# Moving the pool of the experts' tiles up by 128 bytes in SBUF

## The chip, the cores and the metric

The kernel runs on one core of one Trainium2 chip. The metric is the device time of one execution in microseconds (us); a comparison takes the median of several runs. Engines are called as the profile calls them: PE is TensorE's matmul, PEld its weight load, DVE is VectorE, ACT is ScalarE, POOL is GpSimd, SP is SyncE, whose queue issues the DMAs.

## The reference

Two decoder layers over 256 tokens of 1024 channels, then a final RMSNorm. Each layer has four groups of attention heads behind one input projection, an output projection, and a SwiGLU channel mixer: dense in layer 0, eight experts with the two best of them for each token in layer 1. The part that the change touches is the mixture:

```
logits = (xt @ router).astype(jnp.float32)
top_v, top_i = lax.top_k(logits, TOP_K)
gates = jax.nn.softmax(top_v, axis=-1)
...
y = (jax.nn.silu(xb @ w1[e]) * (xb @ w3[e])) @ w2[e]
return y * g[:, None].astype(y.dtype)
```

`w1` and `w3` of an expert are 1024 x 3584, `w2` is 3584 x 1024, all fp32: the eight experts have 352 MB of weights.

## The kernel before

Every product of fp32 operands is made of three matmuls. Each operand is split in a high part (rounded to the format that PE multiplies in one pass) and a low part (what is left), and high x high, high x low and low x high are summed in PSUM. `mm3` (L453 to L456) issues the three: `o, lh, rh`, then `o, lh, rl`, then `o, ll, rh`, the first operand stationary, the second moving. Since the trace names the operands as moving, then stationary, `acc<-wh,g` is a matmul in which a split weight `wh` streams past a stationary `g`.

The weights are split on the core. `Stream` (L217 on) loads units of 1 MB from HBM into tiles `raw`; for each half of one, a piece of 128 x 1024, ACT copies it to a tile `wh` (L305) and DVE subtracts that from `raw` into `wl` (L306). There are five `wh` and five `wl` tiles, and up to fifteen `raw` slots. A load is issued as soon as a `raw` slot is free; a piece is split up to four ahead of the matmuls that read it (`MAHEAD`).

The work of the experts is 56 steps, 8 experts by 7 blocks of 512 hidden channels. Stationary in the experts are small tiles of the pool `moe` (called `mp`, L1013): `g` holds the high and low part of the tokens gathered for an expert (128 slots), `th` and `tl` the hidden block transposed; `sT` holds the expert's slots to put the results back, `yy` the expert's output, `hd` and `sg` the hidden block. One step is

- `g1`: the gate and the up product, 4 pieces each, 6 matmuls of 512 columns on a piece (`acc<-wh,g`, `acc<-wl,g`); ahead of the up product `hidden` transposes the block of the step before with four small matmuls (`tp<-cst,hd`, L1239);
- `g2`: the down product of the step before, 4 pieces, 6 matmuls of 512 columns on each (`mm<-wh,th`, `mm<-wl,th`, `mm<-wh,tl`).

That is 72 matmuls of 512 columns a step. Once for each expert come two bursts of gather matmuls (L1187) and a transposition in `back`, and four scatters of two matmuls each (`tp<-yy,sT`, L1292) from the expert before. The order of all this is written out by hand: the layers and the experts run in the order of the program on each engine.

SBUF is laid out by pools, one after the other from the low end: `rawp`, `hp` (the `wh`), `lp` (the `wl`), `com` (constants and small tiles), then in layer 1's mixture `mp` and `ms` (small statistics). Other pools stand at the high end, among them `big` with `xh` and `xl`, the split activations of the layers. `com` holds a tile `fill` that nothing reads (L1388); its size decides where the tiles behind it begin. In the built program the byte addresses in a partition are:

```
tiles                                   start      modulo 512   modulo 256
wh, wl (all ten)                        74368 ...     128          128
xh, xl (stationary or moving, layers)  188288 ...     384          128
cTh, cTl (stationary, layers)          133120 ...       0            0
th, tl of the dense mixer (moving)     165632 ...     256            0
cst (identity for transposes)          115456         256            0
g of the experts, both buffers         117504 ...     256            0
th, tl of the experts                  174848 ...     256            0
```

A matmul reads whole blocks of these tiles, at steps of 512 bytes or a multiple, so a tile's place modulo 256 is that of every operand cut from it, but for the 416-column products of the layers.

Two functions issue nearly all matmuls in question: `mm3` for those in the experts and in the layers' `proj_nat` (moving `wh`, stationary `xh`: the same shape and order as in the experts, with `xh` in place of `g`), and `accumulate` and the loops of `g1` in `ffn0` for the dense mixer, where the weights are stationary and 256 columns of `xh` or `th` move.

Of the kernel before, what the change touches and what calls it, by code (L numbers as in the profile page):

```python
# [24 lines left out]
F32 = mybir.dt.float32  # L25
# [302 lines left out]
def trunk(ctx, tc, a, out, stop=None):  # L328
# [7 lines left out]
    com = ctx.enter_context(tc.tile_pool(name="com", bufs=1, reuse_waits="tile"))  # L336
# [1048 lines left out]

    rg = com.tile([128, KC, E], F32, name="rg")
    trib = com.tile([128, 128], BF, name="trib")
    com.tile([128, 8], F32, name="fill")  # L1388
    onesb = com.tile([128, 1], BF, name="onesb")
    pool.memset(onesb, 1.0)  # L1390
    ffn0()
# [55 lines left out]
```

## Time and profile before

| what | value |
|---|---|
| three runs | 1491.73, 1489.2, 1486.29 us; median 1489.2 us |
| the profiled execution's own time | 1487.16 us |
| its span on the core | 1485.0 us |
| mean granted TensorE clock | 0.994 |
| busy: PE, PEld, DVE, ACT, POOL | 99%, 84%, 83%, 71%, 2% of the span |
| chain that ended last | PE 96% |
| layer 0 with the dense mixer | about 0 to 320 us |
| attention of layer 1 | about 320 to 455 us |
| the experts and the final norm | from about 455 us to the end |

A matmul's own duration in the trace (395 ns for 512 columns) reaches past the start of the next one, since matmuls are pipelined. What a matmul costs in a stream is the distance from its start to the next start; it is read from the starts in the view in order of time. Rows of that view have the start in us, the duration in us, the engine, line, operation, operands, array size and moving shape.

### The profile page before, as it was taken

What the parts mean: (1) busy time and instruction counts of PE and PEld (TensorE: products, weight loads), DVE (VectorE), ACT (ScalarE), POOL (GpSimd) and SP (SyncE); (2) the same over time, 40 slices, a digit from 0 to 9 for tenths busy, and PEclk for the clock granted to TensorE, in tenths of its full rate; (3) what the DMA queues carried; (4) which work ended last, traced back from release to release, by engine and by line L of the source; (5) the groups of instructions that cost most, each with busy time, mean ns of one, the idle gap of its engine ahead of it and who ended that gap; (6) DMA issues with size and microseconds to landing.
All of it is one profiled execution on the core that took longest, in us unless ns stands there. A gap on an engine that the chain in (4) does not pass through costs nothing.

```text
span 1485.0 us, 21467 instructions
## 1 busy us (share of the span) xinstructions
PE 1464.4 (99%) x8092; PEld 1254.0 (84%) x8092; DVE 1229.9 (83%) x1574; ACT 1047.0 (71%) x1387; POOL 31.9 (2%) x38
## 2 busy tenths in 40 slices
PE   9999999999999999999999999999999999999996
PEld 7999999999997788888888888888888888888885
DVE  6766655666756998998998999899899989989996
ACT  6666444455656877777777777778787777777774
POOL 2001000010000100000000000000000000000000
PEclk9999999999999999999999999999999999999998
DMA  9723555366538798999999999899999999999770
GB/s 368 290 86 135 182 179 191 135 217 223 187 117 317 306 381 303 347 367 331 361 349 339 354 350 370 324 352 362 336 357 354 360 330 346 366 332 360 235 256 31
DMA packets 62334, 426.36 MB, mean 287 GB/s; under 512 B 7176, under 2 KB 7824, under 8 KB 13712
## 3 DMA queue, kind: packets, MB, share of 16 engines
q1 hardware_dynamic: 62224, 424.92, 78.2%
q8 instruction: 65, 1.06, 0.3%
q14 instruction: 45, 0.37, 0.1%
HBM read 423.85 MB, written 1.05 MB: 286 GB/s over the span
## 4 chain that ended last, share of the span: by engine, by line
PE 96%; DVE 1%; ACT 1%; DMA 0%; issue 0%; SPq 0%; POOL 0%; ACTq 0%; POOLq 0%
PE acc L454 14%; PE acc L456 14%; PE acc L455 14%; PE mm L454 7%; PE mm L456 7%; PE mm L455 7%; PE B L972 3%; PE B L971 3%; PE B L970 3%; PE A L522 2%; PE A L523 2%; PE A L524 2%; PE tp L1187 2%; PE tp L1239 2%; PE A L594 2%; PE A L595 1%
## 5 line engine op out<-in xcount | busy, mean ns | idle before, releaser
L306 DVE TENSOR_TENSOR wl<-raw,wh 128x1024 fp32r<-128x1024 f32 (+2 forms) x801 | 970.8, 1224 | 155.9 <-ACT wh L305 152.6
L305 ACT ACTIVATE wh<-raw 128x1024 fp32r<-128x1024 f32 (+2 forms) x801 | 844.5, 1057 | 301.5 <-PE acc L456 123.3
L454 PE MATMUL acc<-wh,g 128*128 128x512 f32 x896 | 360.3, 402 | 0.0
L455 PE MATMUL acc<-wl,g 128*128 128x512 f32 x896 | 353.9, 395 | 0.3 <-DVE wl L306 0.3
L456 PE MATMUL acc<-wh,g 128*128 128x512 f32 x896 | 354.2, 395 | 0.0
L456 PEld LDWEIGHTS acc<-wh,g 128*128 128x128 f32 x896 | 169.1, 189 | 39.5
L455 PEld LDWEIGHTS acc<-wl,g 128*128 128x128 f32 x896 | 169.5, 189 | 36.9 <-DVE wl L306 0.7
L454 PEld LDWEIGHTS acc<-wh,g 128*128 128x128 f32 x896 | 169.4, 189 | 36.2
L454 PE MATMUL mm<-wh,th 128*128 128x512 f32 x440 | 173.8, 395 | 0.0
L456 PE MATMUL mm<-wh,tl 128*128 128x512 f32 x440 | 173.7, 395 | 0.0
L455 PE MATMUL mm<-wl,th 128*128 128x512 f32 x440 | 173.6, 395 | 0.0
L456 PEld LDWEIGHTS mm<-wh,tl 128*128 128x128 f32 x440 | 82.8, 188 | 19.6 <-DVE tl L460 0.3
L455 PEld LDWEIGHTS mm<-wl,th 128*128 128x128 f32 x440 | 82.9, 188 | 19.5
L454 PEld LDWEIGHTS mm<-wh,th 128*128 128x128 f32 x440 | 82.9, 188 | 19.3
L972 PE MATMUL B<-xh,wl 128*128 128x256 f32 x336 | 95.2, 283 | 0.0
L970 PE MATMUL B<-xh,wh 128*128 128x256 f32 x336 | 95.1, 283 | 0.0
L971 PE MATMUL B<-xl,wh 128*128 128x256 f32 x336 | 95.1, 283 | 0.0
L970 PEld LDWEIGHTS B<-xh,wh 128*128 128x128 f32 x336 | 64.5, 192 | 0.0
L972 PEld LDWEIGHTS B<-xh,wl 128*128 128x128 f32 x336 | 64.5, 192 | 0.0
L971 PEld LDWEIGHTS B<-xl,wh 128*128 128x128 f32 x336 | 64.5, 192 | 0.0
L594 PE MATMUL A<-xh,wh 128*128 128x256 f32 x176 | 51.4, 292 | 0.0
L596 PE MATMUL A<-xh,wl 128*128 128x256 f32 x176 | 49.7, 283 | 0.0
(256 smaller groups left out, 1745.8 us busy)
## 6 DMA issues: line engine op xcount, KB each, us to landing
raw<-in_wmoe SPq DMA_DIRECT2D x324, 1024.0 KB, 6.0
raw<-in_wt SPq DMA_DIRECT2D x53, 1024.0 KB, 4.9
raw<-in_wmoe SPq DMA_DIRECT2D x24, 512.0 KB, 4.9
ac<-in_att SPq DMA_DIRECT2D x2, 1728.0 KB, 8.5
raw<-in_wt SPq DMA_DIRECT2D x5, 512.0 KB, 4.7
raw<-in_wt SPq DMA_DIRECT2D x2, 960.0 KB, 14.6
raw<-in_wt SPq DMA_DIRECT2D x2, 928.0 KB, 8.6
raw<-in_wt SPq DMA_DIRECT2D x2, 832.0 KB, 9.0
```

Source lines behind the costliest of these rows:

```text
L305: nc.scalar.activation(h[:, sl], raw[:, sl], AF.Copy)
L306: nc.vector.tensor_sub(l[:, sl], raw[:, sl], h[:, sl].bitcast(F32))
L454: pe.matmul(o, lh, rh, start=start, stop=False, **kw)
L455: pe.matmul(o, lh, rl, start=False, stop=False, **kw)
L456: pe.matmul(o, ll, rh, start=False, stop=stop, **kw)
L522: pe.matmul(o, wh[wsl], h, start=s0, stop=False, skip_group_check=True)
L523: pe.matmul(o, wh[wsl], lo, start=False, stop=False, skip_group_check=True)
L594: pe.matmul(o, hv[:, k], xh[:, k], start=k == 0, stop=False)
L596: pe.matmul(o, lv[:, k], xh[:, k], start=False, stop=k == KC - 1)
L970: pe.matmul(o, hv[:, k], xh[:, k], start=k == 0, stop=False)
L971: pe.matmul(o, hv[:, k], xl[:, k], start=False, stop=False)
L972: pe.matmul(o, lv[:, k], xh[:, k], start=False, stop=k == KC - 1)
```

## The change

The tile `fill` in the pool `com` gets 40 numbers instead of 8, so 160 bytes instead of 32 in each partition.

```diff
     trib = com.tile([128, 128], BF, name="trib")
-    com.tile([128, 8], F32, name="fill")
+    com.tile([128, 40], F32, name="fill")
     onesb = com.tile([128, 1], BF, name="onesb")
```

All that stands behind it at the low end moves up by 128 bytes: `onesb`, every tile of `mp` (`g` to 117632, `th` to 174976, so 128 modulo 256 and 384 modulo 512, and with them `yy`, `xx`, `xnh`, `xnl`, `hd`, `oh`, `sg`, `sT`, `tl` and three early `raw` slots) and every tile of `ms`. `wh`, `wl`, `cst`, the regular `raw` tiles and everything of the layers and the dense mixer stay where they are. No instruction is added, removed or moved on any engine; only addresses differ.

## Rows read from the trace of the kernel before

**Rows 1.** The page, busy us of an engine, share of the span, instructions.
```profile
PE 1464.4 (99%) x8092; PEld 1254.0 (84%) x8092; DVE 1229.9 (83%) x1574; ACT 1047.0 (71%) x1387; POOL 31.9 (2%) x38
```

**Rows 2.** Busy us by stretch (instructions), then granted clock, DMA share, GB/s.
```profile
500.00:1400.00 900.00, 899.69 (x4115) 735.69 (x4114) 831.05 (x817) 705.89 (x776) 5.75 (x2) 1.00 0.94 344
```

**Rows 3.** Waits from 500 to 1400 us: us in total, times, longest.
```profile
ACT wh L305 <- PE acc L456: 111.6, 328, 0.9
ACT wh L305 <- PE mm L456: 73.0, 200, 0.8
DVE wl L306 <- ACT wh L305: 59.9, 330, 0.6
...
PE acc L455 <- DVE wl L306: 0.3, 1, 0.3
```

**Rows 4.** PE in order of time, one step of an expert: first and last matmuls.
```profile
910.75 0.60 PE L1239 MATMUL tp<-cst,hd 128*128 128x128 f32 x4
911.11 0.48 PE L454 MATMUL acc<-wh,g 128*128 128x512 f32 x1
911.42 0.39 PE L455 MATMUL acc<-wl,g 128*128 128x512 f32 x1
...
927.93 0.60 PE L1239 MATMUL tp<-cst,hd 128*128 128x128 f32 x4
```

**Rows 5.** Groups by line and shape: count, busy us, mean ns.
```profile
L454 PE MATMUL acc<-wh,g 128*128 128x512 f32 x896 | 360.3, 402 | 0.0
L454 PE MATMUL mm<-wh,th 128*128 128x512 f32 x440 | 173.8, 395 | 0.0
L1239 PE MATMUL tp<-cst,hd 128*128 128x128 f32 x224 | 33.6, 272 | 0.3 <-DVE hd L1261 0.3
```

**Rows 6.** PE in order of time, layer 1, 512-column products on xh.
```profile
326.59 0.39 PE L454 MATMUL A<-wh,xh 128*128 128x512 f32 x1
...
331.81 0.39 PE L456 MATMUL A<-wh,xl 128*128 128x512 f32 x1
```

**Rows 7.** The same product, its last piece after a pause.
```profile
333.61 0.40 PE L455 MATMUL A<-wl,xh 128*128 128x512 f32 x1
...
335.93 0.39 PE L456 MATMUL A<-wh,xl 128*128 128x512 f32 x1
```

**Rows 8.** PE in order of time, layer 0, 512 columns on cTh.
```profile
45.36 0.39 PE L454 MATMUL A<-wh,cTh 128*128 128x512 f32 x1
...
46.06 0.33 PE L454 MATMUL A<-wh,cTh 128*128 128x384 f32 x1
```

**Rows 9.** Groups by line and shape, DVE: count, busy us, mean ns, idle.
```profile
L306 DVE TENSOR_TENSOR wl<-raw,wh 128x1024 fp32r<-128x1024 f32 x787 | 957.5, 1229 | 147.3 <-ACT wh L305 144.0 <-PE B L873 1.1 <-issue 0.3
L1261 DVE SCALAR_TENSOR_TENSOR hd<-acc,rsl,sg 128x512 f32<-128x512 f32 x56 | 41.7, 745 | 1.0 <-PE acc L456 1.0
L460 DVE TENSOR_TENSOR tl<-tp,th 128x512 fp32r<-128x512 f32 x55 | 37.6, 684 | 1.5 <-ACT th L459 1.5
L1296 DVE SCALAR_TENSOR_TENSOR xx<-tp,gate,xx 128x512 f32<-128x512 f32 x32 | 23.7, 745 | 1.4 <-PE tp L1292 1.4
L475 DVE TENSOR_TENSOR xT<-A,xT 128x512 f32<-128x512 f32 x12 | 8.1, 684 | 1.5 <-PE A L524 1.3
```

**Rows 10.** Waits of SP's DMA queue from 500 to 1400 us.
```profile
SPq L292 <- DVE wl L306: 757.8, 290, 9.3
```

**Rows 11.** SP's DMA queue in order of time: the last loads of weights.
```profile
1426.28 15.72 SPq L292 DMA_DIRECT2D raw<-in_wmoe  x10
```

**Rows 12.** The page, GB/s in 40 slices of the span.
```profile
GB/s 368 290 86 135 182 179 191 135 217 223 187 117 317 306 381 303 347 367 331 361 349 339 354 350 370 324 352 362 336 357 354 360 330 346 366 332 360 235 256 31
```

**Rows 13.** PE in order of time, dense mixer, 256 columns: th moves, then xh.
```profile
243.52 0.28 PE L522 MATMUL A<-th,wh 128*128 128x256 f32 x1
...
249.22 0.28 PE L970 MATMUL B<-xh,wh 128*128 128x256 f32 x1
...
254.97 0.28 PE L970 MATMUL B<-xh,wh 128*128 128x256 f32 x1
```

## The prediction

> **What bounds the kernel now.** I read the page's busy shares first: PE is busy for 99% of the span [rows 1]. Then the experts, by the stretch from 500 to 1400 us: PE 899.69 of 900 us, DVE 831 (92%), ACT 706, the DMA engines 94% [rows 2]. Who waits for whom settles it: ACT's copy of the weights waits 184.6 us for PE to release `wh` (111.6 + 73.0), DVE waits 59.9 us for ACT, and PE waits 0.3 us for DVE [rows 3]. So in the experts PE sets the pace, and a microsecond that PE saves there is one off the end, until DVE or the loads get in the way. The change can only act on how fast operands are read or written, for no instruction moves; the question is what a matmul costs.
>
> That is read from starts. In an ordinary step 72 matmuls of 512 columns and four transposes take 927.93 - 910.75 = 17.18 us; from the second matmul to the next transposes are 71 distances in 927.93 - 911.42 = 16.51 us, so 232.5 ns each [rows 4]. In layer 1 the same routine (`mm3`, `wh` moving, 512 columns) runs on `xh` instead of `g`: two pieces in a row, 24 matmuls, start from 326.59 to 331.81 us, 23 distances in 5.22 us, 227.0 ns each [rows 6]. The printed starts leave 0.4 ns of doubt. Shape, order, clock and moving tiles are the same; the stationary one stands at 128 modulo 256 (384 modulo 512) for `xh`, as `wh` does modulo 256, and at 0 (256 modulo 512) for `g`. A third product has its stationary operand at 0 too, `cTh` in layer 0, in the quieter part of the kernel: three matmuls of 512 columns from 45.36 to 46.06 us, 233 ns each [rows 8]. So 232 ns is no mark of the busy experts, and the place of the stationary operand against the moving one is the simplest thing that sorts the three.
>
> The pace of 227 ns is not there at once. Layer 1's last piece comes after a pause: from 333.61 to 335.93 us are ten distances of 232 ns [rows 7]. Some ten matmuls after a restart still go at the old pace, so I count a run as fast only from its eleventh matmul.
>
> **The change part by part.**
>
> *The products on `g`, `th`, `tl`.* Their stationary tiles come to 128 modulo 256 and 384 modulo 512, just where `xh` is against `wh`. Matmuls of 512 columns: 56 steps x 72 = 4032 (3 x 896 on `acc` and 3 x 440 on `mm` are in their groups, the last step's 24 in another) [rows 5]. Restarts: seven `hidden` transpositions for each expert, two bursts of gathers, one `back`, so ten, on 8 experts 80; at ten slow matmuls each, 800. Left are 3232, at 232.5 - 227.0 = 5.5 ns: 17.8 us. Bounds: nothing, if the place does not matter; 4032 x 5.5 = 22.2 us if no restart costs anything; below zero as in the third rival. I take 17.8, the value at the nearest row, for shape and order there are those of the experts.
>
> *The transposes of `hd`.* `hd` now stands elsewhere than the identity `cst` beside it, which stays at 0. There are 224 of them [rows 5]; if each lost or won the whole 5.5 ns, it would be 1.2 us either way. I take 0. Gathers and scatters have both operands in the moved pool and keep their relation.
>
> *DVE and ACT on the moved tiles.* DVE's 128x512 subtraction with `th`, at place 0, takes 684 ns, and its 128x512 addition with `xT`, at place 128, 684 ns [rows 9]. No difference, so 0. `raw` slots in the moved pool serve three loads, six of some 800 pieces; a tenth more or less on each 1.229 us is under 0.8 us and off the path.
>
> *What is late next.* DVE's work in a step: 12 x 1.229 + 0.745 + 0.684 = 16.18 us [rows 9]. PE's step becomes 17.18 - 62 x 0.0055 = 16.84 us. DVE fits by 0.66 us instead of 1.00. Two steps of seven are tighter. With the scatters DVE has 4 x 0.745 = 2.98 us more, PE 8 x 0.227 = 1.8 us; with the split of the expert's output DVE has 2 x 0.684 = 1.37 us more: 0.5 and 0.7 us short, 1.2 for each expert. Pieces are split up to four ahead, 4 x 6 x 0.227 = 5.4 us, and a split takes ACT and DVE some 2.3 us, so the shortfall is covered. If that cover failed, 8 x 1.2 = 9.6 us would come back.
>
> *The loads.* They need the 344 GB/s of rows 2 to rise by 2%, to 351; single slices of the page show 381, 370 and 367 [rows 12]. The queue waits for a slot that DVE has to release, 757.8 of 900 us [rows 10], and the last ten loads are issued by 1442 us, 43 us ahead of the end [rows 11]. Even at the old rate that lead would hold a gain of 18 us.
>
> The Trainium skill, "SBUF — State Buffer", section "A bandwidth-pool intuition that's wrong (but worth ruling out)", puts HBM at about 358 GB/s for a core. As a hard ceiling it would leave the loads 2% of room above 351 and so would not stop this change either, only the next one. The 381 GB/s of a slice [rows 12] goes past it, so the trace does not agree with a ceiling there.
>
> **Sum.** On the profiled execution: 1487.16 - 17.8 = 1469.4 us. That execution lies 2.0 us under the median of the three runs (1489.2), which themselves differ by 5.4; I put the forecast between 1469.4 and 1471.4, at 1470 us.
>
> **The rivals.**
>
> *The gain is had only in part.* Runs in the experts fall out of the fast pace oftener than ten times for an expert, or DVE's two tight steps hold PE up (the 9.6 us above). For it: DVE is at 92% and goes to 94% [rows 2]. Against: PE waits 0.3 us for DVE in 900 [rows 3]. Half of the gain: 1489.2 - 9 = about 1480 us.
>
> *Nothing happens.* The place does not decide the pace; the 24 matmuls of rows 6 are fast for another reason, such as that the loads were few there or that `xh` does not come from the just written pool. For it: only one long run shows the pace. Against: rows 8, slow in an early and quiet part with `cTh` at 0. Then 1489 us, give or take the 2.7 us of the three runs. The Trainium skill, "TensorE: Matmul & The Clock Gate", section "Part 2: What happens when you issue a matmul", speaks for this rival: it says that PE reads the moving operand and the next weights through two independent ports, so that a weight load takes nothing from the running matmul. By that rule no place could cost anything, and the sum would be 0. The trace has two paces, 232.5 and 227.0 ns, for one shape at one clock [rows 4, 6], which the rule leaves unexplained.
>
> *Slower: sharing a place costs.* In the dense mixer 48 matmuls of 256 columns with `th` moving, at 0 against weights at 128, go from 243.52 to 249.22 us, 118.75 ns each; the next 48, with `xh` moving at the same place modulo 256 as the weights, to 254.97, 119.8 ns each [rows 13]. There sharing is the slower by 1.05 ns. If that held in the experts and went with the columns, 2 x 1.05 x 4032 = 8.5 us more: 1498 us. It decides if the distance in an ordinary step comes out above 232.5 ns. Against it: the row with 512 columns itself says the opposite [rows 6], and at 256 columns a weight load of 128 columns (PEld, busy 84% [rows 1]) is nearly as long as the matmul, so the two cases need not go alike.
>
> **How the numbers follow.** What a measurement of this kernel can tell from no change is about 0.3%, 4.5 us. The forecast has 0.70, its own range 1464 (all matmuls fast) to 1478; the part gain 0.08; no change 0.12; slower 0.10. Faster by over 0.3%: 0.70 + 0.08 = 0.78; within: 0.12; slower: 0.10. The range from 1463 to 1488 takes in the forecast, the part gain and the lower half of no change, and leaves out under 2 in 10.
>
> **What would show it.** Right: in the experts of the new profile PE's starts lie 227 ns apart from some ten matmuls after each `hidden` on, an ordinary step takes 16.8 us, and ACT's 184.6 us of waiting for PE shrink while DVE's share rises towards 94%. The layers and the dense mixer must read as now. The part gain would show waits of PE for `wl` or a mixture of the two paces. Wrong: 232 ns as before (the place is not the cause), or more (the third rival).

## The result and the profile after

The changed kernel takes 1469.62 us in the median of four runs (1469.33 to 1470.91), the kernel before 1489.89; the ratio is 0.9869, with a 95% interval of 0.9849 to 0.9889. Forecast were 1470 us. The profiled execution took 1470.91 us with a span of 1468.7, against 1487.16 and 1485.0. Of one kernel of the experiments, `e10_place32`, two of eight executions took 1793 and 6101 us, and its time is the median of the other six.

An ordinary step of the experts, PE in order of time (start in us, duration, engine, line, operation), answers to [rows 4]:

```profile
958.72 0.60 PE L1239 MATMUL tp<-cst,hd 128*128 128x128 f32 x4
959.08 0.48 PE L454 MATMUL acc<-wh,g 128*128 128x512 f32 x1
959.39 0.40 PE L455 MATMUL acc<-wl,g 128*128 128x512 f32 x1
...
961.70 0.39 PE L456 MATMUL acc<-wh,g 128*128 128x512 f32 x1
...
975.54 0.60 PE L1239 MATMUL tp<-cst,hd 128*128 128x128 f32 x4
```

The step is 975.54 - 958.72 = 16.82 us, where it was 17.18. Behind the transposes ten distances take 961.70 - 959.39 = 2.31 us, 231 ns each; the 61 from there to the next transposes take 13.84 us, 226.9 ns each. So the new pace sets in just as in layer 1: slow for some ten matmuls [rows 7], then fast [rows 6].

The durations show it less plainly: a single one is printed as 0.39 or 0.40 us at either pace, and the mean for `mm<-wh,th` goes from 395 ns [rows 5] to 391:

```profile
L454 PE MATMUL mm<-wh,th 128*128 128x512 f32 x440 | 171.9, 391 | 0.0
```

The rest of the experts follows, by stretch (busy us and instructions of PE, PEld, DVE, ACT, POOL, then clock, DMA share, GB/s) and by waits (us in total, times, longest), against [rows 2, 3]:

```profile
500.00:1400.00 900.00, 899.55 (x4193) 747.61 (x4192) 842.61 (x833) 720.18 (x790) 5.76 (x2) 1.00 0.94 349
```

```profile
ACT wh L305 <- PE acc L456: 96.6, 303, 1.0
ACT wh L305 <- PE mm L456: 67.3, 204, 0.8
...
DVE wl L306 <- ACT wh L305: 16.2, 71, 0.6
...
PE acc L455 <- DVE wl L306: 0.4, 1, 0.4
```

In the same 900 us stand 4193 matmuls instead of 4115. ACT waits 163.9 us for PE instead of 184.6, DVE 16.2 for ACT instead of 59.9, and is busy for 842.6 us, 93.6%. PE's wait for DVE stays at 0.4 us. DVE and the moved tiles show no change, against [rows 9]:

```profile
L306 DVE TENSOR_TENSOR wl<-raw,wh 128x1024 fp32r<-128x1024 f32 x787 | 953.6, 1229 | 133.0 <-ACT wh L305 95.6 <-PE B L873 1.1 <-issue 0.3
L460 DVE TENSOR_TENSOR tl<-tp,th 128x512 fp32r<-128x512 f32 x55 | 37.6, 684 | 1.5 <-ACT th L459 1.5
```

The experts' first product and the last scatter, before, after, and in the second profile of the changed kernel, taken with the experiments (`after_again`):

```profile
460.04 0.73 PE L454 MATMUL acc<-wh,g 128*128 128x512 f32 x1
...
1473.37 0.75 PE L1292 MATMUL tp<-yy,sT 128*128 128x512 f32 x2 [0.18 <-DVE yy L460]
```

```profile
462.12 0.73 PE L454 MATMUL acc<-wh,g 128*128 128x512 f32 x1
...
1457.47 0.73 PE L1292 MATMUL tp<-yy,sT 128*128 128x512 f32 x2 [0.16 <-DVE yy L460]
```

```profile
462.48 0.73 PE L454 MATMUL acc<-wh,g 128*128 128x512 f32 x1
...
1456.99 0.73 PE L1292 MATMUL tp<-yy,sT 128*128 128x512 f32 x2 [0.17 <-DVE yy L460]
```

That is 995.35 us after and 1013.33 before: 17.98 us less. In `after_again` it is 994.51 us, 18.82 less. The two differ by where PE ran at the lower clock (a granted clock of 0.50, so 1.2 GHz). By stretch, after:

```profile
1440.60:1443.90 3.30, 3.30 (x10) 2.52 (x9) 1.95 (x3) 1.06 (x1) 0.00 (x0) 0.50 0.00 0
454.50:464.30 9.80, 9.06 (x38) 8.65 (x38) 5.21 (x18) 4.75 (x13) 0.70 (x1) 0.50 1.01 426
```

and before:

```profile
454.50:464.30 9.80, 9.49 (x44) 8.61 (x45) 5.86 (x18) 5.35 (x14) 0.70 (x1) 0.65 1.01 428
1454.00:1462.00 8.00, 8.00 (x45) 6.54 (x44) 6.71 (x7) 3.98 (x5) 0.00 (x0) 1.00 0.00 0
```

Ahead of the stretch at 454.50 PE had stood idle for the routing (2 us before L1073). After, it began earlier: the gathers ahead of the experts took 1.6 us more than before and lie outside the 17.98 us, which is why the profiled spans differ by only 16.3; and it slowed five of the experts' first products, where it slowed eight before and in `after_again`. Ahead of the stretch at 1440.60 PE ran sixteen matmuls of only eight rows (`acc<-gfin,cst`, L1147). It lies inside the 17.98 us and cost some eight matmuls at 427 instead of 227 ns, 1.6 us. In `after_again` the clock after those sixteen stayed at 1.00, as before, so its 18.82 us are the cleaner measure of the change.

### The profile page after: what moved, and what is told of

It is laid out like the page before. It is cut to its first block, busy times and chain, and to the rows that moved or that the text cites. A ratio compares the mean times of both kernels' runs of the same rounds, so it can differ in the third digit from the quotient of the medians.

```text
span 1468.7 us, 21467 instructions
## 1 busy us (share of the span) xinstructions
PE 1448.2 (99%) x8092; PEld 1253.7 (85%) x8092; DVE 1225.0 (83%) x1574; ACT 1047.2 (71%) x1387; POOL 31.8 (2%) x38
## 4 chain that ended last, share of the span: by engine, by line
PE 96%; DVE 1%; ACT 1%; issue 1%; DMA 1%; SPq 0%; POOL 0%; ACTq 0%; DVEq 0%; POOLq 0%
PE acc L454 14%; PE acc L456 14%; PE acc L455 14%; PE mm L454 7%; PE mm L455 7%; PE mm L456 7%; PE B L972 3%; PE B L971 3%; PE B L970 3%; PE A L522 2%; PE A L523 2%; PE A L524 2%; PE tp L1187 2%; PE tp L1239 2%; PE A L594 2%; PE A L595 1%
## 5 line engine op out<-in xcount | busy, mean ns | idle before, releaser
L454 PE MATMUL acc<-wh,g 128*128 128x512 f32 x896 | 357.1, 399 | 0.0
L455 PE MATMUL acc<-wl,g 128*128 128x512 f32 x896 | 350.0, 391 | 0.4 <-DVE wl L306 0.4
L456 PE MATMUL acc<-wh,g 128*128 128x512 f32 x896 | 350.1, 391 | 0.0
L595 PE MATMUL A<-xl,wh 128*128 128x256 f32 x176 | 49.7, 283 | 0.0
```

The source lines that it names most:

```text
L454: pe.matmul(o, lh, rh, start=start, stop=False, **kw)
L455: pe.matmul(o, lh, rl, start=False, stop=False, **kw)
L456: pe.matmul(o, ll, rh, start=False, stop=stop, **kw)
L595: pe.matmul(o, hv[:, k], xl[:, k], start=False, stop=False)
```

## The experiments

Ten kernels ask which property of the place makes the pace; the ordinary step between two `tp<-cst,hd` measures it, and the whole time stands beside it. Each is the kernel before with the edit shown. The medians of the kernel before, measured beside them, were 1489.1 to 1489.3 us.

**Two more places.** The fill tile makes the place of the pool.

```diff
-    com.tile([128, 8], F32, name="fill")
+    com.tile([128, 24], F32, name="fill")    # e1_place64
+    com.tile([128, 56], F32, name="fill")    # e2_place192
```

> The pool of the experts' tiles stands 64 bytes higher than before (g, th, tl at 64 modulo 256, wh and wl at 128). Theory (a product is fast when its moving and its stationary operand stand at the same place modulo 256): not the same place, so no fast pace; an ordinary step's distance between starts 230 to 233 ns, time about 1489 us. Rival (the cost grows with the distance between the two places): half the distance of before, so about 229.5 ns and 1480 us.

> The pool stands 192 bytes higher than before (g, th, tl at 192 modulo 256, 64 above wh). Theory (same place modulo 256 or slow): 230 to 233 ns, about 1489 us. Rival (cost by distance, either sign): as at 64, about 229.5 ns and 1480 us.

Measured: 1477.4 us at 64 (ratio 0.9923, 0.9907 to 0.994) and 1493.39 us at 192 (1.0025, 1.0015 to 1.0036). One ordinary step of each, first the place 64, then 192:

```profile
908.43 0.60 PE L1239 MATMUL tp<-cst,hd 128*128 128x128 f32 x4
...
925.36 0.60 PE L1239 MATMUL tp<-cst,hd 128*128 128x128 f32 x4
```

```profile
896.71 0.60 PE L1239 MATMUL tp<-cst,hd 128*128 128x128 f32 x4
...
913.96 0.60 PE L1239 MATMUL tp<-cst,hd 128*128 128x128 f32 x4
```

16.93 and 17.25 us. The theory falls at 64, where there is a third pace between the two; the rival came near there (229.5 ns and 1480 us forecast), but falls at 192, where the same distance above `wh` is slower than the kernel before. What matters has a sign.

**Modulo 256 or 512.** The pool 256 and 384 bytes higher.

```diff
-    com.tile([128, 8], F32, name="fill")
+    com.tile([128, 72], F32, name="fill")    # e3_plus256
+    com.tile([128, 104], F32, name="fill")   # e4_plus384
```

> The pool stands 256 bytes higher than before: g at 0 modulo 256 as before, but at 0 instead of 256 modulo 512. Theory (the place modulo 256 decides): as before, 232.5 ns in an ordinary step, 1489 us. Rival (another position in SBUF, whichever, was what helped, or the place modulo 512 decides): about 227 ns and 1470 us.

> The pool stands 384 bytes higher than before: g at 128 modulo 256 as in the changed kernel, but at 128 instead of 384 modulo 512, which is also where wh stands modulo 512. Theory (modulo 256): as the changed kernel, 227 ns after some ten matmuls from a restart, 1470 us. Rival (modulo 512: the two operands have to stand 256 bytes apart, as in the changed kernel and for xh): 232 ns, 1489 us.

Measured: 1488.49 us (0.9997, 0.9987 to 1.0006) and 1470.95 us (0.9881, 0.9865 to 0.9898). The steps, at 256 and at 384:

```profile
912.07 0.60 PE L1239 MATMUL tp<-cst,hd 128*128 128x128 f32 x4
...
929.25 0.60 PE L1239 MATMUL tp<-cst,hd 128*128 128x128 f32 x4
```

```profile
903.50 0.60 PE L1239 MATMUL tp<-cst,hd 128*128 128x128 f32 x4
...
920.32 0.60 PE L1239 MATMUL tp<-cst,hd 128*128 128x128 f32 x4
```

17.18 and 16.82 us, the old and the new step again. The pattern repeats every 256 bytes, and the move as such did nothing.

**The other operand moved.**

```diff
+    padp = ctx.enter_context(tc.tile_pool(name="padp", bufs=1, reuse_waits="tile"))
+    padp.tile([128, 32], F32, name="pad")
     hp = ctx.enter_context(tc.tile_pool(name="hp", bufs=NHL, reuse_waits="tile"))
...
-    com.tile([128, 8], F32, name="fill")
+    com.tile([128, 40], F32, name="fill")
```

> The other operand is moved instead: a pad of 128 bytes ahead of the pool of wh puts wh and wl at 0 modulo 256, and the pool of the experts' tiles stays at 0 modulo 256. xh of the layers stays at 128, so it loses its relation to wh, and th of the dense mixer gains it. Theory (the relation of the two operands decides): the experts as in the changed kernel, 227 ns, 18 us less; layer 1's 512-column products on xh go to 232 ns (96 matmuls, 0.5 us more); the dense mixer's 256-column products with xh moving go from 119.8 to about 118.8 ns (some 1900, 2 us less) and those with th from 118.8 to 119.8 (528, 0.6 us more): about 1470 us. Rival (the experts' tiles themselves have to stand at 128): 232.5 ns and 1489 us.

Measured: 1469.21 us (0.9863, 0.9847 to 0.988). Its experts, then layer 1's 512 columns on `xh`, then the dense mixer with `th` and with `xh` moving (lines are two further on):

```profile
902.21 0.60 PE L1241 MATMUL tp<-cst,hd 128*128 128x128 f32 x4
...
919.03 0.60 PE L1241 MATMUL tp<-cst,hd 128*128 128x128 f32 x4
...
322.74 0.39 PE L456 MATMUL A<-wh,xh 128*128 128x512 f32 x1
...
330.90 0.39 PE L458 MATMUL A<-wh,xl 128*128 128x512 f32 x1
...
242.71 0.28 PE L524 MATMUL A<-th,wh 128*128 128x256 f32 x1
...
248.45 0.28 PE L972 MATMUL B<-xh,wh 128*128 128x256 f32 x1
...
254.15 0.28 PE L972 MATMUL B<-xh,wh 128*128 128x256 f32 x1
```

The experts' step is 16.82 us though none of their tiles stands at 128. In layer 1, 35 distances take 8.16 us, 233 ns, where [rows 6] had 227. In the dense mixer `th` now takes 5.74 us for 48 matmuls and `xh` 5.70, where [rows 13] had 5.70 and 5.75. Each of these products changed with its relation to `wh`, and in the forecast direction. This settles it: the relation decides, not the tile's own place, and the experts need not be busy or quiet for it.

The same run says that [rows 8] were no evidence. `cTh` shares the place of `wh` here, and its three products of 512 columns are no faster: 45.33 to 46.03 us, 0.70 as in [rows 8]. Three products are too few to tell the places apart, for the first ten are slow at the same place too [rows 7].

```profile
45.33 0.39 PE L456 MATMUL A<-wh,cTh 128*128 128x512 f32 x1
...
46.03 0.33 PE L456 MATMUL A<-wh,cTh 128*128 128x384 f32 x1
```

**One part alone.** Only `th` and `tl` moved.

```diff
+                        if not pad:
+                            pad.append(mp.tile([128, 32], F32, name="pad"))
                         th = mp.tile([128, 4, 128], F32R, name="th")
```

> One part alone: a pad of 128 bytes inside the experts' pool, ahead of th, moves only th and tl to 128 modulo 256; g and all else stay at 0. Theory: only the down products (mm, 24 matmuls a step) go to 227 ns, after some ten matmuls from the change over from acc, and acc stays at 232.5: 56 x 14 x 5.5 ns = 4.3 us less, about 1485 us; 7.4 us less, 1482, if the pace changes at once. Rival (it is another tile of the pool, such as hd, yy or xnh, that counts): mm stays at 232.5 ns, 1489 us.

Measured: 1482.61 us (0.9958, 0.9941 to 0.9974), 6.7 us less, near the bound for a pace that changes at once. The first and the last of 24 down products, and the first product after them:

```profile
915.96 0.39 PE L454 MATMUL mm<-wh,th 128*128 128x512 f32 x1
...
921.17 0.40 PE L456 MATMUL mm<-wh,tl 128*128 128x512 f32 x1
921.41 0.40 PE L454 MATMUL acc<-wh,g 128*128 128x512 f32 x1
```

23 distances in 5.21 us, 226.5 ns, from the first on, between products on `acc` that keep the old pace. So it is `th` and `tl` for the down products, and `g`, which stayed, for those on `acc`. A change of operand can be free, but is not always: of the 47 runs of 24 down products, 37 are fast from the first on, and ten have seven to thirteen slow distances. Seven of these ten come where the down products begin 18 products behind the transposition in `back`, here nine distances in 2.09 us, 232 ns:

```profile
954.29 0.40 PE L454 MATMUL mm<-wh,th 128*128 128x512 f32 x1
...
956.38 0.39 PE L454 MATMUL mm<-wh,th 128*128 128x512 f32 x1
```

**The ring filled in.** Four more places, in steps of 32 bytes.

```diff
-    com.tile([128, 8], F32, name="fill")
+    com.tile([128, 32], F32, name="fill")    # e8_place96
+    com.tile([128, 48], F32, name="fill")    # e9_place160
+    com.tile([128, 16], F32, name="fill")    # e10_place32
+    com.tile([128, 64], F32, name="fill")    # e11_place224
```

> The pool stands 96 bytes higher than before (g, th, tl at 96 modulo 256, 32 below wh). Measured so far: 64 below wh 229 ns and 1477.4 us, at wh 226.7 ns and 1470.0 us, 64 above 233.4 ns and 1493.4 us, 128 off 232.4 ns and 1489 us. Theory (a pace for each distance, smooth between): about 227.8 ns and 1474 us. Rival (a restart is cheaper below wh, as it was at 64, and the pace is that of the same place): about 226.7 ns from the first matmuls on and 1466 us.

> The pool stands 160 bytes higher than before (g, th, tl at 160 modulo 256, 32 above wh). Theory (a pace for each distance, smooth between 226.7 ns at wh and 233.4 ns at 64 above): about 230 ns and 1481 us. Rival (only the exact place is fast, on the upper side): 233 ns and 1492 us.

> The pool stands 32 bytes higher than before (g, th, tl at 32 modulo 256, 96 below wh). Theory after the runs so far (every distance has a pace of its own and no neighbour tells it; only the same place and 64 below were under 230 ns): a slow pace of 232 to 234 ns, 1489 to 1494 us. Rival (the side below wh is the better one, 32 below an exception): 230 ns, about 1481 us.

> The pool stands 224 bytes higher than before (g, th, tl at 224 modulo 256, 96 above wh). Theory: a slow pace of 232 to 234 ns, 1489 to 1494 us. Rival (an exception like 64 below wh stands on this side too): 229 to 230 ns, about 1479 us.

Steps of the first two, 32 below `wh` (17.23 us) and 32 above (17.23 us):

```profile
913.98 0.60 PE L1239 MATMUL tp<-cst,hd 128*128 128x128 f32 x4
...
931.21 0.60 PE L1239 MATMUL tp<-cst,hd 128*128 128x128 f32 x4
```

```profile
896.90 0.60 PE L1239 MATMUL tp<-cst,hd 128*128 128x128 f32 x4
...
914.13 0.60 PE L1239 MATMUL tp<-cst,hd 128*128 128x128 f32 x4
```

With all the runs, by the stationary tile's place minus that of `wh`, modulo 256:

| difference | kernel | ordinary step, us | time, us | ratio to before |
|---|---|---|---|---|
| 0 | changed kernel | 16.82 | 1469.62 | 0.9869 |
| +32 | e9_place160 | 17.23 | 1493.05 | 1.0021 (1.001 to 1.0032) |
| +64 | e2_place192 | 17.25 | 1493.39 | 1.0025 |
| +96 | e11_place224 | 17.30 | 1495.86 | 1.0046 (1.003 to 1.0062) |
| 128 | before | 17.18 | 1489.89 | 1 |
| -96 | e10_place32 | 17.23 | 1494.2 | 1.0033 (1.0021 to 1.0044) |
| -64 | e1_place64 | 16.93 | 1477.4 | 0.9923 |
| -32 | e8_place96 | 17.23 | 1492.91 | 1.0027 (1.0018 to 1.0037) |

The smooth curve is refuted: 32 below and 32 above the best place are both slower than the kernel before. Two places of the eight tried are good, and no neighbour tells which. Places between these steps were not tried, and `wh` and `wl` always shared one.

**A version meant to beat both.** The changed kernel with `xh` and its neighbours at 0, for the 256-column products.

```diff
-    edge.tile([128, 24], F32, name="edge")
+    edge.tile([128, 56], F32, name="edge")
...
+    trp.tile([128, 32], F32, name="pad")
```

> The changed kernel, and besides xh, xl, oTh, oTl (and the raw slots beside them) moved from 128 to 0 modulo 256 by a larger tile at the high end and a pad; th of the dense mixer, cTh and the experts' tiles keep their places. Theory (for matmuls of 256 columns the same place is the slower one, for 512 columns the faster): as the run with wh at 0 showed for the layers, the 256-column products with xh or oTh moving win 1.2 + 0.4 + 0.3 us, the 96 matmuls of 512 columns on xh lose up to 0.5 us; the experts stay as they are: 1.5 us less than the changed kernel in the same call, about 1468 us. Rival (the split of raw tiles that now stand at 0 while wh and wl stand at 128 gets slower on DVE, 1229 ns before): no gain, 1470 us or more.

> The changed kernel once more, to stand beside the run with xh at 0 on one chip: 1470 us by every theory.

Measured: 1469.34 us (1467.99 to 1471.09) and 1470.87 us (1470.27 to 1471.88), ratios to before 0.987 and 0.9877. The 1.5 us are as forecast, but the runs overlap, so the times don't prove them. The starts do show the cause at work: over all products of 256 columns with `xh`, `xl`, `oTh` or `oTl` moving, the distances add up to 249.83 us, where `after_again` has 251.83. With `xh` moving, 48 matmuls take 5.69 us instead of 5.75:

```profile
248.05 0.28 PE L971 MATMUL B<-xh,wh 128*128 128x256 f32 x1
...
253.74 0.28 PE L971 MATMUL B<-xh,wh 128*128 128x256 f32 x1
```

## Why the prediction was right

*PE sets the pace of the experts.* It held: PE waits 0.4 us for DVE after, 0.3 before, and what the matmuls saved came off the end.

*The place of the stationary against the moving operand.* It held, and the run with `wh` moved shows it was the relation. But it rested on one run of 24 matmuls [rows 6] against the experts, for [rows 8], which the prediction held against "nothing happens", are three distances of 232 ns, and stay at 233 where `cTh` shares the place [e5_wh_at_0]; it could have been chance. The forecast was no more than "the same relation gives the same pace", and that much is true. What the prediction did not know is that every other distance has a pace of its own: had the pool gone up by 96 bytes instead of 128, the kernel would have become 3.6 us slower [e8_place96].

*The term of 17.8 us.* Measured between first product and last scatter: 17.98, or 18.82 in `after_again`. Of 4032 distances, counted over the starts, 3329 are under 228 ns, where 3232 were forecast. The 80 restarts cost fewer than ten slow matmuls each in the mean: 21 of the 56 runs behind `hidden` are only six products long, and behind the gathers the slow distances are 112, where 160 were forecast; 43 slow ones behind scatters and the final norm's matmuls were not counted. The fast pace is 226.6, not 227.0, which is within the 0.4 ns of doubt. 3329 x (232.4 - 226.6) = 19.3 us.

*The time of 1470 us.* That it is met to 0.4 us is in part luck. The forecast went out from an execution of 1487.16 us; the medians fell by 20.3 us in the result, and by 18.2 where both kernels were timed again [after_again].

*The terms set to zero.* Over the starts, the 224 transposes of `hd` take 19.9 us before and 19.8 after; DVE's subtraction stayed at 684 ns. DVE's two tight steps were covered: it rose to 93.6%, and PE's waits for it did not grow beyond the 0.4 us. The loads rose to 349 GB/s and their lead held.

*The rivals.* No change fell with the first trace. "Sharing a place costs" was right where its row stood: at 256 columns the same place is the slower in the run with `wh` at 0 too. It was wrong to carry it to 512 columns, as the prediction judged; one of its reasons is off, though, for at 256 columns the weight load is not nearly as long as the matmul (192 ns against 283 in the profile). The Trainium skill ("TensorE: Matmul & The Clock Gate", "Part 2: What happens when you issue a matmul") gives PE two independent read ports, so that loading the next weights takes nothing from the running matmul. By that rule no place would have cost anything; the trace does not agree, with steps of 16.82 to 17.30 us at one clock (1.00). What a matmul costs hangs on the two addresses together; why was not tried and stays open.

## What to carry to other kernels

On a kernel that PE bounds, read the distance between the starts of equal matmuls, for each pair of operands apart: two paces for one shape were worth more than a percent here, and single durations in the profile hide them. Then look at the addresses of the stationary and the moving tile modulo 256, and try the places all the way round in steps of 32 bytes with a pad, for here the curve was not smooth. Pads and odd small tiles between pools are not neutral: a change that grew a tile elsewhere made this matmul-bound kernel up to 1.3% faster or 0.5% slower through the addresses alone. Only this kernel was tried.

## What was not expected

The pace is a repeating pattern, not noise. At 128 apart the distances of 230, 232 and 241 ns come again in the same order step after step; at the same place they settle at 226 and 227, behind `hidden` after about ten matmuls, behind most scatters at once, under the same load of DVE, ACT and DMA. For 256 columns the order of good and bad is the reverse of that for 512 (118.75 ns at 128 apart, 119.8 at the same place). There the weight loads show it too: those for `xh` moving take 192 ns before, at the same place, and 188 with `wh` moved; for `th` it is 188 and 191. In the experts they stay at 187 to 189 ns, at the fast places and the slow. Before, then with `wh` moved:

```profile
L970 PEld LDWEIGHTS B<-xh,wh 128*128 128x128 f32 x336 | 64.5, 192 | 0.0
L522 PEld LDWEIGHTS A<-th,wh 128*128 128x128 f32 x176 | 33.2, 188 | 0.0
```

```profile
L972 PEld LDWEIGHTS B<-xh,wh 128*128 128x128 f32 x336 | 63.3, 188 | 0.0
L524 PEld LDWEIGHTS A<-th,wh 128*128 128x128 f32 x176 | 33.7, 191 | 0.0
```

Why 64 below is good and 32 below is not stays open.
